# Triangular blocks through one load, their off-diagonal product in place, and a neighbour level inside a burst of small matmuls

## The chip, the cores and the metric

The kernel runs on one core of a Trainium2 chip. The metric is the device time of one execution in microseconds (us). A profile is one profiled execution: every instruction of TensorE (PE, with its weight loads PEld), VectorE (DVE), ScalarE (ACT), GpSimd (POOL) and every DMA issue on SyncE's queue (SPq), with start and duration.

## The reference

One decoder layer over 1024 prompt tokens and 8 sample tokens, all in float32. Cut to what the change touches:

```python
p = x @ w_in                                    # 1024 -> 9360 columns: GLA, RWKV-7, gates
# GLA (4 heads, keys 128, values 256): gated linear attention, in chunks
A = einsum('bhid,bhjd,bhijd->bhij', q, k, decay)   # decay = exp(b_i - b_j) for j <= i
o = A @ v + (q * exp(b)) @ S
# RWKV-7 (16 heads of 64): one state update per token
S = S * w_t + (S @ -kk_t) (kk_t * a_t)^T + v_t k_t^T ;  y_t = S @ r_t
...
m = sigmoid(gate_a) * (o_gla @ w_up_gla) + sigmoid(gate_b) * (o_rwkv @ w_up_rwkv)
y = layernorm(alpha * x + m @ w_out)
```

## The kernel before

The tokens go through in two passes of 512 (the 8 sample tokens ride with the first). The bulk of TensorE's work is `x @ w_in`: blocks of 128 columns, 24 matmuls each for a token tile, with x and w split into a rounded high and a low part (tiles `xs`, `wpart`, results in the PSUM tags `proj`, `big`, `pY`). Between these stand the two recurrences as side streams:

- RWKV (8 pairs of heads a pass, 16 in all): `pair` runs `front`, `back`, `turn`, `chain`, `norm`. A chunk of 64 tokens needs the inverse of a unit lower triangular 64x64 matrix. It is built from 32x32 blocks: the diagonal blocks of `GG` go to DRAM (`LD`) and come back as `L`, one matrix to a partition; VectorE solves them by 31 steps on `X`/`Xt`; the results go out to `XD` and come back as the diagonal of `XT` and as `X2`. The lower left block is a product of three: the off-diagonal block of `GG` (here carried by own transfers into `L1`), the transposed first inverse (`X1`, in which VectorE puts transposes into a zeroed block diagonal), and the second inverse (`X2`). The two products are the matmuls `big<-X,L` (out of it comes `A`) and `big<-X,A`.
- GLA (4 heads a pass, 8 in all): `gla_head` builds the 128x128 attention of a chunk by levels 1, 2, 4, ... 64: at level m, queries and keys that lie m apart. Level 0 (a token with itself) and level 1 (its neighbour) are products on VectorE, summed by a transpose and a reduce into `pair` tiles; levels 2 to 32 are 40 matmuls with 32 stationary columns in one burst (`big<-row`, 80 rows in a profile, since a float32 matmul shows as two), out of which predicated copies pick into `AC`.

The order on every engine is set when the program is built, by a greedy planner (`Order.run`): every stream offers its next operation, the planner's own costs say which could start first, priorities break ties, and each engine then executes its list in order. Any edit of a stream so moves the operations of all others a little. All DMAs are issued from one queue, SyncE's, in that order. The buffers are the tags of the table `SBUF` with a count each; `E.` operations may go to VectorE or GpSimd, `C.` operations to ScalarE or VectorE, as the planner sees fit. `slow` adds to the landing time that the planner reckons with; `together` issues several matmuls as one operation, its second argument scaling the planned cost.

Of the kernel before, what the change touches and what calls it, by code (L numbers as in the profile page):

```python
# [15 lines left out]
ALU = mybir.AluOpType  # L16
AP = bass.AP
# [3 lines left out]
P = 128  # L21
# [5 lines left out]
HT = TP // 2  # L27

PASS = [(0, HT + NS, NS, [(0, 256), (256, 264)]), (HT + NS, HT, 0, [(0, 512)])]
GH, GDK, GDV = 4, 128, 256  # L30
RH, RN = 16, 64
NPAIR = RH // 2
C = 64
NCH = HT // C
GC = 128
NGC = HT // GC
# [11 lines left out]
    "l2s": ([P, 2 * P], 1), "pc": ([P, NCH], 3), "X": ([P, 256], 1),  # L48
    "Xt": ([P, P], 1), "L1": ([P, P], 1), "A": ([P, P], 1), "S": ([P, GDV], 2), "Sp": ([P, C], 2), "s0p": ([P, C], 2), "rh": ([P, P], 2),
    "sto": ([P, P], 1), "az": ([P, 2 * HT], 2), "bnd": ([P, 1], 3), "st": ([P, 32], 3), "part": ([P, HALF], 2), "l2p": ([P, 2 * P], 2),  # L50
    "pair": ([P, 2, HT // 32], 3), "nst": ([P, 2 * NCH], 2), "ac": ([P, HT // 4], 1),
}
# [47 lines left out]
_o = 0  # L100
for _n, _w in [("ident", 128), ("gmask", 256)]:
    CST[_n] = (_o, _w)
    _o += _w
# [10 lines left out]
def constants():  # L114
    c = np.zeros((P, CST_W), np.float32)

    def put(name, v):
        o, w = CST[name]
        c[:, o:o + w] = v

    i = np.arange(P)
    put("ident", np.eye(P))
    s, t = i[:, None] % C, i[None, :] % C
    put("gmask", np.concatenate([s < t, s <= t], axis=1))
    j = np.arange(2 * B32) % B32
    lev = np.concatenate([i[:, None] % B32 // m == j // m for m in LEVELS[:MASKED]], axis=1).astype(np.uint8)
    return c, lev, ((i[:, None] // C) == (i[None] // C)).astype(np.float32)
# [295 lines left out]
class Kern(Order):  # L423
# [72 lines left out]
    def setup(self):  # L496
        nc, a = self.nc, self.a
        E = mybir.EngineType
# [59 lines left out]

        for tag, n, bufs in (("XT", 2 * HT, 2), ("X1", HT, 1), ("X2", HT, 1)):
            ts = [cp.tile([P, n], F32, name=f"{tag}{i}") for i in range(bufs)]  # L560
            for t in ts:
                nc.gpsimd.memset(t, 0.0)
            self.fixed(tag, ts)
# [235 lines left out]
    def gla_head(self, c, h, rows, g):  # L799
# [26 lines left out]
        u, w = z[:, :HT], vk1[:, :HT]  # L826
        r, r2, dd = yield from self.get("pair", 3)
        yield E.tensor_mul(u.rearrange("p (a e q) -> p a q e", e=2, q=GC), self.paired(q), self.paired(k))
        yield E.tensor_mul(qp_, qp_, al[:, :HT])
        yield V.transpose(w, u)  # L830
        yield V.tensor_reduce(r[:, 0], self.blocks32(w), mybir.AxisListType.X, ALU.add)
        half, four, two = NGC // 2, (4, HT // 4), [(2 * GC, NGC // 2), (2, GC // 2)]
        yield E.tensor_mul(self.strided(u, 0, *two, (GC + 1, 2)),
                           self.strided(km_, 0, (2 * GC, half), (4, GC // 2), (3, 2)),
                           self.strided(qp_, 2, (2 * GC, half), (4, GC // 2), (-1, 2)))
        yield V.transpose(w, u)
        yield V.tensor_reduce(r[:, 1], self.blocks32(w), mybir.AxisListType.X, ALU.add)
        b = [slice(32 * i, 32 * i + 32) for i in range(4)]
        for i in (0, 2):
            yield V.tensor_add(r2[b[i]], r[b[i]], r[b[i + 1]])  # L840
        for i in range(4):
            yield V.tensor_add(dd[b[i], :, 0:NGC], r2[b[0], :, i::4], r2[b[2], :, i::4])
        d0, d1 = (dd[:, i, 0:NGC].rearrange("p (a e) -> p a e", e=2).unsqueeze(2) for i in range(2))
        AC = yield from self.get("ac")
# [5 lines left out]
                                d0.to_broadcast([P, half, B32, 2]))  # L850
        yield V.copy_predicated(self.strided(AC, 2, (2 * B32, half), (4, B32 // 2), (-1, 2)),
                                eye.rearrange("p (b e) -> p b e", e=2).unsqueeze(1).to_broadcast([P, half, B32 // 2, 2]),
                                d1.to_broadcast([P, half, B32 // 2, 2]))
        self.free(r, r2, dd)
        kept = [z, vk1, *(yield from self.rows(2))]
        tot, pl = al[:, :HT], None
        small, mms = [m for m in LEVELS if 1 < m < B32], []
        for lv, m in enumerate(LEVELS):
# [8 lines left out]
            elif m == B32:  # L867
# [13 lines left out]
                for lo, y in enumerate(small):  # L881
                    yield V.copy_predicated(self.strided(AC, 2 * y, (4 * y, B32 // y), (1 - 2 * y, 2), (2, y)),
                                            lev[:, lo + 1].rearrange("p (b e m) -> p b e m", e=2, m=y),
                                            pl[:, lo].rearrange("p x (b e m) -> p (x b) e m", e=2, m=y))
# [250 lines left out]
    def front(self, c, p, st, d):  # L1135
# [80 lines left out]
        X = X_.rearrange("p (i t) -> p i t", t=32)  # L1216
        yield E.memset(X, 0.0)
        for q in range(4):
            yield E.memset(X_[NU * q:NU * q + NU, q::36], 1.0)
        for q in range(4):  # L1220
            yield slow(self.S.dma_start(L_[NU * q:NU * q + NU], LD.rearrange("n c s t -> (n c) (s t)")), 1.0)
        tm = yield from self.get("Xt")
# [12 lines left out]
        for q in range(4):  # L1235
            yield slow(self.S.dma_start(XD.rearrange("u (i g) t -> g u i t", g=4)[q], X[NU * q:NU * q + NU]), 0.5)
        self.free(X_)

        L1 = (yield from self.get("L1")).rearrange("p (x t) -> p x t", t=32)
        X2 = (yield from self.get("X2")).rearrange("p (g t) -> p g t", t=P)  # L1240
        H = NCH // 2
        for h in range(2):
            for n in range(2):
                g = 2 * h + n
                yield slow(self.S.dma_start(L1[32 * g:32 * g + 32], GG[64 * h:64 * h + 32, H * n:H * n + H, 0, h, 32:64]), -0.5)
        for q in range(2):
# [8 lines left out]
        d.AZ, d.BK, d.G, d.XT, d.v, d.bonus, d.pc, d.L, d.L1, d.X2 = AZ, BK, GG, XT, st[2], st[1], pc, L_, L1, X2  # L1255

    def back(self, d):
        GG, XT = d.G, d.XT

        H = NCH // 2  # L1260
        X1 = (yield from self.get("X1")).rearrange("p (x t) -> p x t", t=P)
        q = [slice(32 * n, 32 * n + 32) for n in range(4)]
        for h in range(2):
            for n in range(2):
                g = 2 * h + n
                yield self.V.transpose(X1[q[g], :, q[g]], XT[q[2 * h], H * n:H * n + H, h, 0:32])
# [575 lines left out]
```

## Time and profile before

| | us |
|---|---|
| median of 3 runs (lowest to highest) | 1476.96 (1476.38 to 1477.36) |
| the profiled execution | 1478.35 |
| its span, from the first to the last instruction | 1476.5 |
| PE busy in it | 1446.6 |
| DVE busy | 1163.0 |
| ACT busy | 878.9 |
| POOL busy | 108.8 |

The profiled execution took 1.85 us more than its span and 1.39 us more than the median of the runs. Nearly all operations are recorded by one helper line (L217), so a row is told by its tiles: `out<-in`, buffer numbers left out. A shape such as `128*32 128x32` in a PE row is the part of the array (rows*columns) and the operand moved (partitions x elements). "busy" counts time covered by any instruction of a group once; "mean ns" is the length of one instruction, which for pipelined matmuls is more than the time from one to the next.

### The profile page before, as it was taken

The page shows a single profiled execution, that of the slowest core. Times are in us where ns is not written, and L with a number is a line of the kernel's source. Part 1 is how long each engine was busy: PE and PEld are TensorE (multiplying, and loading weights), DVE is VectorE, ACT ScalarE, POOL GpSimd, SP SyncE. Part 2 cuts the span into 40 slices and gives each one's busy share as a digit, 9 for nine tenths or more (in the row PEclk, how much of TensorE's full clock was granted, in tenths as well). Part 3 has the DMA queues.
Part 4 walks back from the last instruction along what each step waited for, and adds up shares of the span by engine and source line. Part 5 has one row for each costly group of instructions (what it writes and reads, how often), then busy time and mean ns, then how long its engine had stood idle before and what let it go on. Part 6 is the DMA issues. An engine that isn't in the chain of part 4 may idle for free.

```text
span 1476.5 us, 31483 instructions
## 1 busy us (share of the span) xinstructions
PE 1446.6 (98%) x11158; PEld 1258.8 (85%) x11158; DVE 1163.0 (79%) x3071; ACT 878.9 (60%) x2302; POOL 108.8 (7%) x205
## 2 busy tenths in 40 slices
PE   9999999999999999999999999999999999999997
PEld 6999989999999998787878777778787899988786
DVE  6697879987899777967998898888876876755665
ACT  5666767775776677655775564465546746643210
POOL 1001010100110001000110210020000000000000
PEclk9999999999999999999999999999999999999999
DMA  8877887669765878548646457656654768987432
GB/s 308 278 260 228 260 268 239 215 212 313 259 240 193 289 259 269 174 140 249 207 131 198 148 160 240 205 153 172 182 172 142 246 196 253 295 300 258 135 109 84
DMA packets 211258, 318.96 MB, mean 216 GB/s; under 512 B 91811, under 2 KB 107180, under 8 KB 211100
## 3 DMA queue, kind: packets, MB, share of 16 engines
q1 hardware_dynamic: 211100, 316.93, 67.1%
q8 instruction: 89, 1.46, 0.4%
q14 instruction: 69, 0.57, 0.1%
HBM read 197.19 MB, written 118.61 MB: 214 GB/s over the span
## 4 chain that ended last, share of the span: by engine, by line
PE 77%; DVE 14%; ACT 3%; DMA 2%; issue 2%; SPq 1%; POOL 0%; POOLq 0%; DVEq 0%; ACTq 0%
PE proj L217 48%; PE big L217 20%; DVE row L217 6%; PE pch L217 5%; PE pY L217 4%; ACT row L217 2%; DVE X L217 1%; DVE wide L217 1%; DVE Xt L217 1%; SPq L217 1%; DVE pair L217 1%; ACT L401 1%; DVE az L217 1%; DVE bk L217 1%; DVE ac L217 1%
## 5 line engine op out<-in xcount | busy, mean ns | idle before, releaser
L217 PE MATMUL proj<-xs,wpart 128*128 128x264 f32 (+2 forms) x5640 | 1022.8, 327 | 1.0 <-DVE row L217 0.8
L217 PEld LDWEIGHTS proj<-xs,wpart 128*128 128x128 f32 x5640 | 811.2, 189 | 82.1 <-issue 10.3
L217 DVE TENSOR_TENSOR row<-row 128x512 f32<-128x512 f32 (+8 forms) x327 | 173.1, 537 | 13.0 <-ACT row L217 6.6
L217 ACT CAST wpart<-wraw 128x512 fp32r<-128x512 f32 x210 | 129.6, 622 | 89.7 <-PE proj L217 36.3
L217 DVE TENSOR_TENSOR wpart<-wraw,wpart 128x512 fp32r<-128x512 f32 x198 | 137.2, 695 | 34.4 <-ACT wpart L217 32.0
L217 ACT ACTIVATE row<-row 128x512 f32<-128x512 f32 (+3 forms) x197 | 117.6, 606 | 13.0 <-DVE row L217 4.1
L217 PE MATMUL big<-xs,wpart 128*128 128x512 f32 (+2 forms) x576 | 102.9, 332 | 0.8 <-DVE xs L217 0.7
L217 DVE TENSOR_TENSOR Xt<-X,wide 128x60 f32<-128x60 f32 (+21 forms) x432 | 94.7, 219 | 9.4
L217 ACT ACTIVATE row<-proj,omu 128x256 f32<-128x256 f32 (+1 forms) x99 | 54.0, 546 | 77.7 <-PE proj L217 77.2
L217 POOL TENSOR_TENSOR row<-row 128x512 f32<-128x512 f32 (+7 forms) x58 | 60.2, 1043 | 536.7 <-DVE row L217 190.5
L217 DVE TENSOR_TENSOR X<-X,Xt 128x60 f32<-128x60 f32 (+21 forms) x432 | 91.8, 212 | 9.7
L217 PEld LDWEIGHTS big<-xs,wpart 128*128 128x128 f32 x576 | 87.0, 191 | 11.9 <-DVE xs L217 1.6
L217 DVE SCALAR_TENSOR_TENSOR wide<-pch,pc,s0p 64x64 f32<-64x64 f32 x208 | 58.8, 283 | 41.6 <-PE pch L217 35.6
L217 ACT COPY rh<-pch 128x128 f32<-128x128 f32 x104 | 27.5, 264 | 84.8 <-PE pch L217 83.8
L401 ACT ACT_TABLE_LOAD x60 | 77.0, 1283 | 1.0
L217 DVE SCALAR_TENSOR_TENSOR row<-proj,pv,row 128x255 f32<-128x255 f32 (+1 forms) x99 | 56.4, 570 | 23.5 <-ACT tail L217 12.3
L217 ACT COPY row<-big 128x128 f32<-128x128 f32 (+7 forms) x144 | 41.1, 308 | 51.5 <-PE big L217 43.2
L217 PE MATMUL big<-row 128*32 128x32 f32 (+4 forms) x944 | 67.3, 243 | 0.8 <-ACT row L217 0.8
L217 ACT COPY row<-wide 64x64 f32<-64x64 f32 x240 | 58.2, 242 | 5.8 <-DVE wide L217 1.8
L217 ACT CAST xs<-row 128x520 fp32r<-128x520 f32 (+1 forms) x64 | 38.4, 622 | 29.2 <-PE proj L217 10.3
L217 PEld LDWEIGHTS pch<-wide,gg 128*128 128x128 f32 x256 | 41.9, 188 | 14.5 <-PE proj L217 5.6
L217 PE MATMUL pch<-wide,gg 128*128 128x128 f32 x256 | 51.2, 281 | 2.9 <-DVE wide L217 1.8
(252 smaller groups left out, 2008.9 us busy)
## 6 DMA issues: line engine op xcount, KB each, us to landing
w<-wpart SPq DMA_DIRECT2D x146, 512.0 KB
wpart<-w SPq DMA_DIRECT2D x146, 512.0 KB
wraw<-w_in SPq DMA_DIRECT2D x146, 256.0 KB
wide<-LD SPq DMA_DIRECT2D x64, 128.0 KB
wraw<-w_up_gla SPq DMA_DIRECT2D x32, 256.0 KB
wraw<-w_up_rwkv SPq DMA_DIRECT2D x32, 256.0 KB
sg<-row SPq DMA_DIRECT2D x16, 260.0 KB
row<-sg SPq DMA_DIRECT2D x16, 260.0 KB
```

The source lines that it names most:

```text
L217: ways.append((eng, lambda call=call: call(out, *args, **kw), price(eng, name, out, args, ins)))
L401: self.nc.scalar.preload_act_table_set(self.table)
```

## The change

1. **One load.** `L` was filled by four loads of the same DRAM matrices, each to 32 partitions, so that partition 32q+u held matrix u for q = 0 to 3. Now one load with a repeat of 4 in its source puts matrix u on partitions 4u to 4u+3, and the stores to `XD` read every fourth partition. The start value of `X`, formerly a memset and four small ones, is a copy of a new constant `unit`, which makes the constants 256 columns wider.
2. **In place.** The tile `L1` and its four transfers per pair go. The product is made by 16 matmuls with 32x32 blocks (before 4 with 128x32) that read the off-diagonal block of `GG` where it stands. `X1` is then a compact 256-column tile without zeroed blocks, filled by two transposes per pair for four, and the result is copied to `A` in two halves out of two banks.
3. **Level 1 in the burst.** `gla_head` drops the VectorE product, transpose, reduce and predicated copy of level 1; the level is two more copies of keys and queries and 8 more matmuls in the burst (48 for 40), with one more predicated copy out of its bank and one more `row` buffer held.

```diff
-for _n, _w in [("ident", 128), ("gmask", 256)]:
+for _n, _w in [("ident", 128), ("gmask", 256), ("unit", 256)]:
...
-        r, r2, dd = yield from self.get("pair", 3)
+        r, dd = yield from self.get("pair", 2)
...
-        yield E.tensor_mul(self.strided(u, 0, *two, (GC + 1, 2)),
-                           self.strided(km_, 0, (2 * GC, half), (4, GC // 2), (3, 2)),
-                           self.strided(qp_, 2, (2 * GC, half), (4, GC // 2), (-1, 2)))
-        yield V.transpose(w, u)
-        yield V.tensor_reduce(r[:, 1], self.blocks32(w), mybir.AxisListType.X, ALU.add)
...
-        yield V.copy_predicated(self.strided(AC, 2, (2 * B32, half), (4, B32 // 2), (-1, 2)),
-                                eye.rearrange("p (b e) -> p b e", e=2).unsqueeze(1).to_broadcast([P, half, B32 // 2, 2]),
-                                d1.to_broadcast([P, half, B32 // 2, 2]))
-        kept = [z, vk1, *(yield from self.rows(2))]
+        kept = [z, vk1, *(yield from self.rows(3))]
-        small, mms = [m for m in LEVELS if 1 < m < B32], []
+        small, mms = [m for m in LEVELS if m < B32], []
...
-        yield E.memset(X, 0.0)
-        for q in range(4):
-            yield E.memset(X_[NU * q:NU * q + NU, q::36], 1.0)
-        for q in range(4):
-            yield slow(self.S.dma_start(L_[NU * q:NU * q + NU], LD.rearrange("n c s t -> (n c) (s t)")), 1.0)
+        yield self.C.copy(X_, self.cst("unit"))
+        yield slow(self.S.dma_start(L_, AP(LD.tensor, LD.offset, [[1024, NU], [0, 4], [1, 1024]])), 1.0)
...
-            yield slow(self.S.dma_start(XD.rearrange("u (i g) t -> g u i t", g=4)[q], X[NU * q:NU * q + NU]), 0.5)
+            yield slow(self.S.dma_start(XD.rearrange("u (i g) t -> g u i t", g=4)[q], X[q::4]), 0.5)
-        L1 = (yield from self.get("L1")).rearrange("p (x t) -> p x t", t=32)
...
-                yield slow(self.S.dma_start(L1[32 * g:32 * g + 32], GG[64 * h:64 * h + 32, H * n:H * n + H, 0, h, 32:64]), -0.5)
...
-        X1 = (yield from self.get("X1")).rearrange("p (x t) -> p x t", t=P)
+        X1 = (yield from self.get("X1")).rearrange("p (c t) -> p c t", t=32)
         for h in range(2):
-            for n in range(2):
-                g = 2 * h + n
-                yield self.V.transpose(X1[q[g], :, q[g]], XT[q[2 * h], H * n:H * n + H, h, 0:32])
-        pA = yield from self.bank("big", [P, P])
-        yield together([self.P.matmul(pA[q[x]], d.L1[:, x], X1[:, x], start=True, stop=True) for x in range(H)])
+            yield self.V.transpose(X1[q[2 * h]], XT[q[2 * h], :, h, 0:32])
+        pA = yield from self.get("big", 2)
+        yield together([self.P.matmul(pA[h][q[x], 32 * n:32 * n + 32], GG[q[2 * h], H * n + x, 0, h, 32:64], X1[q[2 * h], H * n + x],
+                                      start=True, stop=True) for n in range(2) for x in range(H) for h in range(2)], 2.0)
         A_ = yield from self.get("A")
-        yield self.C.copy(A_, pA)
+        for h in range(2):
+            yield self.C.copy(A_[:, C * h:C * h + C], pA[h][:, :C])
```

TensorE, the second pair of the first pass: `big<-X,L` and then `big<-X,gg` is the product that makes `A`, `big<-X,A` the one that follows; `big<-az,bk`, `big<-part,headsr` and `big<-cons,bk` are other steps of the pairs. Before:

```order
L217 MATMUL proj<-xs,wpart 128x264 x6
L217 MATMUL big<-X_173,L_2811 32x128 x4
L217 MATMUL proj<-xs,wpart 128x264 x2
L217 MATMUL big<-az,bk 128x128 x8
L217 MATMUL proj<-xs,wpart 128x264 x12
L217 MATMUL big<-X_175,A 32x128 x4
L217 MATMUL proj<-xs,wpart 128x264 x2
L217 MATMUL big<-row 32x256 x4
```

Now:

```order
L218 MATMUL proj<-xs,wpart 128x264 x22
L218 MATMUL big<-X_2899,gg 32x32 x16
L218 MATMUL proj<-xs,wpart 128x264 x2
L218 MATMUL proj<-xs,wpart 128x256 x9
L218 MATMUL big<-part,headsr 128x512
L218 MATMUL proj<-xs,wpart 128x256 x5
L218 MATMUL big<-X_173,A 32x128 x4
L218 MATMUL big<-part,headsr 128x512
```

Four matmuls became sixteen; some 16 projection matmuls still stand between the two products.

SyncE's queue, the same pair: `XD<-X` stores the solved blocks, `L<-gg` are the four transfers of the off-diagonal block, `XT<-XD` and `X<-XD` load the inverses (`X` is here the tile `X2`), `wraw` and `w_0`/`w_1` are the weights of the projection. Before:

```order
L217 DMA XD_2784<-X 256x1x32 x4
L217 DMA L_2811<-gg 32x4x32 x4
L217 DMA wraw<-w_in 128x512
L217 DMA w_0_2773<-wpart 128x1024
L217 DMA XT_170<-XD_2784 32x8x32 x4
L217 DMA X_175<-XD_2784 32x4x32
L217 DMA wraw<-w_in 128x512
L217 DMA w_1_2898<-wpart 128x1024
L217 DMA X_175<-XD_2784 32x4x32
L217 DMA wraw<-w_in 128x512
L217 DMA w_0_2936<-wpart 128x1024
L217 DMA X_175<-XD_2784 32x4x32 x2
```

Now:

```order
L218 DMA XD_2700<-X 256x1x32 x4
L218 DMA wraw<-w_in 128x512
L218 DMA w_1_2745<-wpart 128x1024
L218 DMA XT_170<-XD_2700 32x8x32 x4
L218 DMA X_173<-XD_2700 32x4x32 x2
L218 DMA wraw<-w_in 128x512
L218 DMA w_0_2862<-wpart 128x1024
L218 DMA X_173<-XD_2700 32x4x32 x2
```

The four transfers are gone, and one weight load with one weight store less stands between the first and the last load of `X2`.

More of the change, by code (lines that the diff above doesn't have):

```diff
@@ L48 @@
     "l2s": ([P, 2 * P], 1), "pc": ([P, NCH], 3), "X": ([P, 256], 1),
-    "Xt": ([P, P], 1), "L1": ([P, P], 1), "A": ([P, P], 1), "S": ([P, GDV], 2), "Sp": ([P, C], 2), "s0p": ([P, C], 2), "rh": ([P, P], 2),
+    "Xt": ([P, P], 1), "X1": ([P, 256], 1), "A": ([P, P], 1), "S": ([P, GDV], 2), "Sp": ([P, C], 2), "s0p": ([P, C], 2), "rh": ([P, P], 2),
     "sto": ([P, P], 1), "az": ([P, 2 * HT], 2), "bnd": ([P, 1], 3), "st": ([P, 32], 3), "part": ([P, HALF], 2), "l2p": ([P, 2 * P], 2),
-    "pair": ([P, 2, HT // 32], 3), "nst": ([P, 2 * NCH], 2), "ac": ([P, HT // 4], 1),
+    "pair": ([P, HT // 32], 2), "nst": ([P, 2 * NCH], 2), "ac": ([P, HT // 4], 1),
 }
@@ L122, in constants @@
     put("ident", np.eye(P))
+    put("unit", np.eye(32).reshape(8, 4, 32).transpose(1, 0, 2).reshape(1, 4, 256).repeat(32, 0).reshape(P, 256))
     s, t = i[:, None] % C, i[None, :] % C
@@ L556, in setup @@
         nc.vector.memset(self.reset[:, ::C], 0)
-        for tag, n, bufs in (("XT", 2 * HT, 2), ("X1", HT, 1), ("X2", HT, 1)):
+        for tag, n, bufs in (("XT", 2 * HT, 2), ("X2", HT, 1)):
             ts = [cp.tile([P, n], F32, name=f"{tag}{i}") for i in range(bufs)]
@@ L830, in gla_head @@
         yield V.transpose(w, u)
-        yield V.tensor_reduce(r[:, 0], self.blocks32(w), mybir.AxisListType.X, ALU.add)
-        half, four, two = NGC // 2, (4, HT // 4), [(2 * GC, NGC // 2), (2, GC // 2)]
-        yield E.tensor_mul(self.strided(u, 0, *two, (GC + 1, 2)),
-                           self.strided(km_, 0, (2 * GC, half), (4, GC // 2), (3, 2)),
-                           self.strided(qp_, 2, (2 * GC, half), (4, GC // 2), (-1, 2)))
-        yield V.transpose(w, u)
-        yield V.tensor_reduce(r[:, 1], self.blocks32(w), mybir.AxisListType.X, ALU.add)
+        yield V.tensor_reduce(r, self.blocks32(w), mybir.AxisListType.X, ALU.add)
+        half = NGC // 2
         b = [slice(32 * i, 32 * i + 32) for i in range(4)]
         for i in (0, 2):
-            yield V.tensor_add(r2[b[i]], r[b[i]], r[b[i + 1]])
+            yield V.tensor_add(r[b[i]], r[b[i]], r[b[i + 1]])
         for i in range(4):
-            yield V.tensor_add(dd[b[i], :, 0:NGC], r2[b[0], :, i::4], r2[b[2], :, i::4])
-        d0, d1 = (dd[:, i, 0:NGC].rearrange("p (a e) -> p a e", e=2).unsqueeze(2) for i in range(2))
+            yield V.tensor_add(dd[b[i], 0:NGC], r[b[0], i::4], r[b[2], i::4])
+        d0 = dd[:, 0:NGC].rearrange("p (a e) -> p a e", e=2).unsqueeze(2)
         AC = yield from self.get("ac")
@@ L850, in gla_head @@
                                 d0.to_broadcast([P, half, B32, 2]))
-        yield V.copy_predicated(self.strided(AC, 2, (2 * B32, half), (4, B32 // 2), (-1, 2)),
-                                eye.rearrange("p (b e) -> p b e", e=2).unsqueeze(1).to_broadcast([P, half, B32 // 2, 2]),
-                                d1.to_broadcast([P, half, B32 // 2, 2]))
-        self.free(r, r2, dd)
-        kept = [z, vk1, *(yield from self.rows(2))]
+        self.free(r, dd)
+        kept = [z, vk1, *(yield from self.rows(3))]
         tot, pl = al[:, :HT], None
-        small, mms = [m for m in LEVELS if 1 < m < B32], []
+        small, mms = [m for m in LEVELS if m < B32], []
         for lv, m in enumerate(LEVELS):
@@ L882, in gla_head @@
                     yield V.copy_predicated(self.strided(AC, 2 * y, (4 * y, B32 // y), (1 - 2 * y, 2), (2, y)),
-                                            lev[:, lo + 1].rearrange("p (b e m) -> p b e m", e=2, m=y),
+                                            lev[:, lo].rearrange("p (b e m) -> p b e m", e=2, m=y),
                                             pl[:, lo].rearrange("p x (b e m) -> p (x b) e m", e=2, m=y))
@@ L1235, in front @@
         for q in range(4):
-            yield slow(self.S.dma_start(XD.rearrange("u (i g) t -> g u i t", g=4)[q], X[NU * q:NU * q + NU]), 0.5)
+            yield slow(self.S.dma_start(XD.rearrange("u (i g) t -> g u i t", g=4)[q], X[q::4]), 0.5)
         self.free(X_)
-        L1 = (yield from self.get("L1")).rearrange("p (x t) -> p x t", t=32)
         X2 = (yield from self.get("X2")).rearrange("p (g t) -> p g t", t=P)
         H = NCH // 2
-        for h in range(2):
-            for n in range(2):
-                g = 2 * h + n
-                yield slow(self.S.dma_start(L1[32 * g:32 * g + 32], GG[64 * h:64 * h + 32, H * n:H * n + H, 0, h, 32:64]), -0.5)
         for q in range(2):
@@ L1254, in front @@
             yield self.S.dma_start(X2[b, :, b], XD[2 * NCH + x::H].rearrange("g s t -> s g t"))
-        d.AZ, d.BK, d.G, d.XT, d.v, d.bonus, d.pc, d.L, d.L1, d.X2 = AZ, BK, GG, XT, st[2], st[1], pc, L_, L1, X2
+        d.AZ, d.BK, d.G, d.XT, d.v, d.bonus, d.pc, d.L, d.X2 = AZ, BK, GG, XT, st[2], st[1], pc, L_, X2
     def back(self, d):
@@ L1260, in back @@
         H = NCH // 2
-        X1 = (yield from self.get("X1")).rearrange("p (x t) -> p x t", t=P)
+        X1 = (yield from self.get("X1")).rearrange("p (c t) -> p c t", t=32)
         q = [slice(32 * n, 32 * n + 32) for n in range(4)]
         for h in range(2):
-            for n in range(2):
-                g = 2 * h + n
-                yield self.V.transpose(X1[q[g], :, q[g]], XT[q[2 * h], H * n:H * n + H, h, 0:32])
-        pA = yield from self.bank("big", [P, P])
-        yield together([self.P.matmul(pA[q[x]], d.L1[:, x], X1[:, x], start=True, stop=True) for x in range(H)])
+            yield self.V.transpose(X1[q[2 * h]], XT[q[2 * h], :, h, 0:32])
+        pA = yield from self.get("big", 2)
+        yield together([self.P.matmul(pA[h][q[x], 32 * n:32 * n + 32], GG[q[2 * h], H * n + x, 0, h, 32:64], X1[q[2 * h], H * n + x],
+                                      start=True, stop=True) for n in range(2) for x in range(H) for h in range(2)], 2.0)
         A_ = yield from self.get("A")
-        yield self.C.copy(A_, pA)
-        self.free(pA, X1, d.L1)
+        for h in range(2):
+            yield self.C.copy(A_[:, C * h:C * h + C], pA[h][:, :C])
+        self.free(*pA, X1)
         pZ = yield from self.bank("big", [P, H, 32])
```

## The prediction

> **What bounds the kernel now.** I read the page first: the busy times, the slices, the chain.
>
> ```profile
> span 1476.5 us, 31483 instructions
> PE 1446.6 (98%) x11158; PEld 1258.8 (85%) x11158; DVE 1163.0 (79%) x3071; ACT 878.9 (60%) x2302; POOL 108.8 (7%) x205
> PE   9999999999999999999999999999999999999997
> PEclk9999999999999999999999999999999999999999
> PE 77%; DVE 14%; ACT 3%; DMA 2%; issue 2%; SPq 1%; POOL 0%; POOLq 0%; DVEq 0%; ACTq 0%
> L217 PE MATMUL proj<-xs,wpart 128*128 128x264 f32 (+2 forms) x5640 | 1022.8, 327 | 1.0 <-DVE row L217 0.8
> ```
>
> TensorE is covered for 1446.6 of 1476.5 us, in every slice but the last, at full clock. Most of that is the projection, whose 5640 matmuls waited 1.0 us in all. The planner puts it wherever a recurrence waits, so a chain that becomes shorter gives nothing by itself. What can change the time is work added to or taken from TensorE, and its idle time: 1476.5 - 1446.6 = 29.9 us. A piece of that is the end of the program. From the timeline of PE, the last row:
>
> ```profile
> 1468.24 0.52 PE L217 MATMUL proj<-wpart,xs 128*128 128x256 f32 x3
> ```
>
> It ends at 1468.8, so 7.7 us are the last layer norm and its stores, which the change leaves alone. Some 22.2 us of waits remain in the whole program. I then asked for the groups by form, and for the timeline around the two products that the change touches:
>
> ```profile
> L217 PE MATMUL big<-X,L 128*32 128x128 f32 x128 | 6.8, 284 | 3.1 <-issue 1.8 <-DVE X L217 1.3
> L217 PE MATMUL big<-X,A 128*32 128x128 f32 x128 | 6.8, 285 | 2.8 <-DMA X<-XD 2.1 <-DVE A L217 0.6
> ```
>
> The two products of the pairs carry 3.1 + 2.8 = 5.9 us of the 22.2. The other 16.3 us are scattered over the rest of the streams.
>
> **The change part by part.** The sum is made against the profiled execution (1478.35 us) and is a difference, which I then put on the median of the runs, 1.39 us lower.
>
> *The burst of GLA (on the path).* Eight matmuls, 16 rows, are added in each of 8 heads. One burst and its successor:
>
> ```profile
> 93.65 0.91 PE L217 MATMUL big<-row 128*32 128x32 f32 x80
> 94.48 3.46 PE L217 MATMUL proj<-xs,wpart 128*128 128x264 f32 x27
> ```
>
> From start to next start 0.83 us for 80 rows, 10.4 ns each. 16 x 10.4 = 0.17 us a head, 8 heads: **+1.3 us**. The new matmuls have the form of those 80, so I give this no range of its own.
>
> *The product that makes A (on the path).* Per pair 8 rows of 128 moved columns go, and 32 rows of 32 moved columns come. The trace has no matmul on 32x32 of the array; these are its neighbours:
>
> ```profile
> 189.27 0.43 PE L217 MATMUL big<-X,L 128*32 128x128 f32 x8
> 189.63 0.51 PE L217 MATMUL proj<-xs,wpart 128*128 128x264 f32 x2
> ...
> 195.02 0.43 PE L217 MATMUL big<-X,A 128*32 128x128 f32 x8 [2.12 <-DMA X<-XD]
> ...
> 196.38 0.71 PE L217 MATMUL big<-cons,bk 64*128 64x64 f32 x16
> 197.02 0.76 PE L217 MATMUL proj<-xs,wpart 128*128 128x264 f32 x4
> ```
>
> Before, 189.63 - 189.27 = 0.36 us. The nearest row is the GLA burst: the same 32 stationary and 32 moved columns, only 128 rows deep for 32. At its 10.4 ns, 32 rows take 0.33 us, 0.03 less, 16 pairs: **-0.5 us**. That is the value I take. The low end: the new form has two row blocks working beside each other where the burst has one, so at half the price 0.17 us, 16 x -0.19 = -3.0. The high end: the 64x64 transposes, a more remote form, take 197.02 - 196.38 = 0.64 us for 16 rows, 40 ns each; 32 of them 1.28 us, 16 x 0.92 = +14.7.
>
> The Trainium skill, "TensorE: Matmul & The Clock Gate", section "Wait — 56ns, not 53.3ns?", says that start-to-start of matmuls never falls below about 25 ns however few columns are moved; by it 32 rows would take 0.8 us and this term would be +7.0 us in place of -0.5 (an estimate from the page's figure). The burst above, at 10.4 ns a row, lies far under that floor, so the trace disagrees for matmuls on different column blocks, and the sum goes by the trace.
>
> *Waits of TensorE on these two products.* The wait of 2.1 us has its cause in SyncE's queue. Its timeline around there, and the tile rows of the DMAs:
>
> ```profile
> 175.42 2.55 SPq L217 DMA_DIRECT2D XD<-X  x4
> 178.02 2.58 SPq L217 DMA_DIRECT2D L<-gg  x4
> ...
> 181.81 2.56 SPq L217 DMA_DIRECT2D XT<-XD  x4
> ...
> 187.94 1.65 SPq L217 DMA_DIRECT2D X<-XD  x2
> L217 SPq DMA_DIRECT2D L<-gg x64: 585/600/1438, 107.9 to 1202.2; - x64
> L217 SPq DMA_DIRECT2D wide<-LD x64: 307/421/1338, 68.9 to 1159.4; - x64
> ```
>
> The four `L<-gg` held the queue for 2.58 us ahead of the loads that the product waited for. With them gone, 64 x 0.600 = 38 us of issue leave the queue, and 48 of the 64 loads of `L`, 48 x 0.421 = 20 us. So the 2.1 us should go. Of the 1.3 us behind `DVE X` I count 0.9 as gained (XT lands earlier and the transposes below are shorter). The 0.6 behind the copy to `A` stays, and the 1.8 of "issue" too, as no row says what they are: **-3.0 us**. Ends: 0, since the order is drawn anew and a load may be late elsewhere, and -5.9, all of it.
>
> *The elementwise work (beside other work).* Rows of the groups by form:
>
> ```profile
> L217 DVE TENSOR_TENSOR row<-row 128x256 f32<-128x256 f32 x119 | 50.8, 440 | 0.8
> L217 DVE STREAM_TRANSPOSE row<-row 128x512 f32<-128x512 f32 x16 | 11.3, 708 | 0.2
> L217 DVE TENSOR_REDUCE pair<-row 128x16 f32<-128x512 f32 x16 | 10.9, 683 | 0.2
> L217 DVE COPY_PREDICATED ac<-lev,pair 128x64 f32<-128x64 uint8 x8 | 2.4, 302 | 0.0
> L217 DVE COPY_PREDICATED ac<-lev,big 128x64 f32<-128x64 uint8 x32 | 9.6, 300 | 0.6
> L217 DVE COPY row<-row 128x256 f32<-128x256 f32 x25 | 6.9, 287 | 0.0
> L217 ACT COPY row<-row 128x256 f32<-128x256 f32 x47 | 19.1, 431 | 17.4 <-DVE row L217 16.9 <-POOL row L217 0.2
> L217 DVE STREAM_TRANSPOSE X<-XT 32x128 f32<-32x128 f32 x64 | 19.2, 300 | 3.0 <-DMA XT<-XD 2.2
> L217 ACT COPY A<-big 128x128 f32<-128x128 f32 x8 | 2.1, 265 | 9.2 <-PE big L217 9.2
> L217 ACT COPY wide<-pch 64x64 f32<-64x64 f32 x160 | 33.0, 206 | 22.9 <-PE pch L217 18.7
> L217 POOL MEMSET X<- 32x8 f32 x60 | 6.3, 105 | 3.1
> L217 POOL MEMSET X<- 128x256 f32 x15 | 5.2, 350 | 37.2 <-DMA XD<-X 37.1
> ```
>
> A head loses 0.440 + 0.708 + 0.683 + 0.302 = 2.13 us and gains a predicated copy of 0.300 and two copies of 0.287 (DVE) or 0.431 (ACT): 1.0 to 1.3 us less, about 9 us over 8 heads. A pair has four transposes of 0.300 for two of 256 columns (between the 300 ns of 128 and the 708 of 512, some 0.44): 0.3 us less, 5 us in all. The copy to `A` is two of about 0.21 for one of 0.265, 16 x 0.15 = 2.4 us more; the copy of `unit` adds 16 x 0.29 to 0.43 to DVE or ACT, some 6 us, and POOL loses 6.3 + 5.2 us. DVE so gives up some 10 of 1163 us. I cost all this at nothing: the projection covers it on TensorE. If that cover were gone, the pair's own path would be 0.15 us longer at the copies and 0.3 shorter at the transposes.
>
> *Other.* The constants are 128 KB larger and are loaded once; GLA and the pairs first need them tens of us later, behind projection. One more `row` of 33 is held in a head: at worst a block waits for a buffer, and the order shows no place where TensorE would stand without projection for it. Both 0.
>
> Sum: 1.3 - 0.5 - 3.0 = -2.2 us. Part of it I expect to see given back: all 16.3 us of the other waits are drawn anew with the order, which helps as often as it harms, so I leave that at 0 and put about 4 us (a quarter of them, an estimate) on either side of the range. Profiled 1478.35 - 2.2 = 1476.1; on the median 1476.96 - 2.2 = **1474.8 us**.
>
> **The rivals.** What a measurement of this kernel can tell from no change is about 0.2%, 3 us.
>
> 1. *Clearly faster*: all 5.9 us of waits go, and the 32x32 rows come at half price: 1.3 - 3.0 - 5.9 = -7.6, so 1469.4 us. For it: the queue loses 58 us of issue, and DVE and POOL have less to do. Against it: three waits of "issue" without a named cause.
> 2. *Slower by the price of small matmuls*: if a 32x32 row costs 40 ns like the 64x64 ones, the product costs +14.7 and the sum is 1.3 + 14.7 - 3.0 = +13.0, 1490.0 us. It decides from about 20 ns a row: 16 x 32 x (20 - 10.4) ns = 4.9 us, which turns -2.2 into +2.7. For it: 512 instructions of a form that the trace does not show. Against it: the burst. By the Trainium skill's floor of about 25 ns from the page named above, the sum would be 1482.3 us.
> 3. *Slower by a new wait*: the order is new, and a load that lands late leaves TensorE standing at a product as it stood 2.1 us at 195.0. Two such and none of the old ones gained: 1.3 - 0.5 + 4.2 = +5.0, 1482.0 us. For it: DVE and the queue are the planner's guesses; against it: 5640 projection matmuls waited only 1.0 us.
> 4. *The change moves nothing*: the freed queue and DVE time is covered as before and the waits stay at 5.9: +0.8, 1477.8 us.
>
> **How the numbers follow.** The forecast, together with rival 4, which lies within its spread: 0.50; rival 1: 0.32; rival 2: 0.08; rival 3: 0.10. A part of the forecast's own spread (0.04) falls below -3 us. So faster 0.36, same 0.45, slower 0.19. The range is from rival 1 with a little beyond, 1468.5, to just short of rival 3, 1481.5; rival 2 lies outside.
>
> **What the profile after would show.** The rows `L<-gg` gone, 16 loads `wide<-LD`; bursts of 96 rows at about 1.0 us to the next start; 512 rows `big<-X,gg`, 0.33 us from a burst's start to the next row; idle before them and before `big<-X,A` under 3 us in sum for 5.9; DVE busy near 1150, POOL near 95. PE's idle total near 27 us. I would be wrong if bursts of 32 take over 0.6 us, or if PE's waits elsewhere grow by more than 4 us.

## The result and the profile after

The changed kernel takes 1466.22 us (median of 6 runs, 1464.59 to 1471.07), the kernel before 1477.16 us beside it (6 runs, 1475.17 to 1478.82). The ratio is 0.9927 [0.9917, 0.9938]: 10.9 us faster, where the forecast was 2.2 us with a range that ended at 1468.5. The forecast was wrong: right in sign, and 8.6 us above the measured time. The profiled execution took 1466.08 us.

From the page of the kernel after (the span, busy times by engine, the costliest group):

```profile
span 1464.1 us, 32120 instructions
PE 1443.8 (99%) x11670; PEld 1261.4 (86%) x11670; DVE 1139.0 (78%) x3022; ACT 888.7 (61%) x2356; POOL 77.7 (5%) x107
...
L218 PE MATMUL proj<-xs,wpart 128*128 128x264 f32 (+2 forms) x5640 | 1018.3, 327 | 1.0 <-DVE row L218 0.8
```

The span is 12.4 us shorter. PE's idle time went from 29.9 to 20.3 us (-9.6), and PE's busy time fell by 2.8 us although it has 512 rows of matmuls more (a float32 matmul shows as two rows). That second figure is not less work, as the accounting below shows. The projection waited 1.0 us, as before. The two products, from the groups by form (busy, mean ns | idle time ahead and what ended it):

```profile
L218 PE MATMUL big<-X,A 128*32 128x128 f32 x128 | 7.2, 285 | 0.5 <-DMA X<-XD 0.5
L218 PE MATMUL big<-X,gg 32*32 32x32 f32 x512 | 6.2, 196 | 0.4 <-DVE X L218 0.4
```

Their idle time is 0.9 us for 5.9. Two bursts and the last row, from the timeline of PE (start, length):

```profile
87.58 1.03 PE L218 MATMUL big<-row 128*32 128x32 f32 x96
88.54 0.63 PE L218 MATMUL proj<-xs,wpart 128*128 128x264 f32 x3
...
183.47 0.35 PE L218 MATMUL big<-X,gg 32*32 32x32 f32 x32
183.75 0.52 PE L218 MATMUL proj<-xs,wpart 128*128 128x264 f32 x2
...
186.62 0.42 PE L218 MATMUL big<-X,A 128*32 128x128 f32 x8 [0.48 <-DMA X<-XD]
...
1455.97 0.52 PE L218 MATMUL proj<-wpart,xs 128*128 128x256 f32 x3
```

From start to next start the GLA burst takes 0.96 us for 96 rows, the new product 0.28 us for 32 rows. Seven of the 8 GLA bursts take 0.96 to 1.01 us and one, with a wait inside, 2.27; of the 16 bursts of the product 13 take 0.28 to 0.29 us, and three have a wait inside (0.46, 0.54 and 0.75 us). The end behind the last projection is as long as before. SyncE's queue, the same pair:

```profile
170.55 2.89 SPq L218 DMA_DIRECT2D XD<-X  x4
...
176.07 1.83 SPq L218 DMA_DIRECT2D XT<-XD  x4
177.95 0.93 SPq L218 DMA_DIRECT2D X<-XD  x2
...
181.09 1.50 SPq L218 DMA_DIRECT2D X<-XD  x2
```

The four `L<-gg` are gone, and the loads of the inverses stand closer behind the stores. Over the 16 pairs, the mean time from the first store to `XD` to the first load of `XT` fell from 6.7 to 4.9 us, and to the start of the first product from 12.9 to 11.7 us.

Five of the larger waits of PE (us in total, times, longest), before:

```profile
PE pch L217 <- DVE wide L217: 3.3, 8, 0.9
PE big L217 <- DMA X<-XD: 2.1, 1, 2.1
...
PE big L217 <- DVE part L217: 1.7, 4, 0.7
...
PE big L217 <- DVE S L217: 1.6, 2, 1.3
...
PE big L217 <- DVE l2p L217: 1.3, 2, 0.9
```

And after:

```profile
PE pch L218 <- DVE wide L218: 1.6, 5, 0.4
PE big L218 <- DVE part L218: 1.4, 2, 1.1
...
PE big L218 <- DVE S L218: 0.4, 1, 0.4
```

Waits shrank in places where the change edits nothing: `pch` and `part` belong to the chain of RWKV, `S` is the state of GLA.

**An account that does not trust "busy".** A matmul's modelled end runs over the next one's start (mean length 406 ns for the widest projection, 232 ns from start to start), so a wait of up to some 0.17 us counts as busy, and a longer one in part. I therefore took every matmul's start from the trace. Its time to the next start, less the usual step of its form (the median where the same form follows, the smaller of the two kernels'), is time lost. Summed, in us:

| | before | after | change |
|---|---|---|---|
| steps at their usual length (the work) | 1331.6 | 1334.6 | +3.0 |
| lost ahead of the two products | 9.3 | 4.0 | -5.3 |
| lost ahead of the pairs' chain (`pch`, `part`, `l2p`) | 25.0 | 17.5 | -7.5 |
| lost between two projections | 50.0 | 47.9 | -2.1 |
| lost elsewhere | 50.9 | 50.4 | -0.5 |
| ahead of the first matmul and from the last one's start | 9.8 | 9.7 | -0.1 |
| span | 1476.5 | 1464.1 | -12.4 |

So the gain is in lost time: 5.3 us at the products that the change edits, 7.5 us at the chain that it does not edit. Not all lost time is a wait that another order would save: between two projections some 42 us, in either kernel, are about 470 steps that are each some 0.09 us too long. What changed most are the long steps: those more than 0.5 us beyond the usual were 29 before, 24.4 us in sum, and are 17 after, 12.7 us. Of the work's +3.0 some 2.2 are bookkeeping: timed as whole bursts, start to next start, the GLA bursts cost 1.0 us more (8 x 0.13) and those of the new product 0.2 less (5.5 us for 5.7), +0.8 in sum, and the difference is credited in the row "elsewhere".

One piece of the loss is the clock. From the windows of the kernel before and, below it, of the kernel after (us, PE, PEld, DVE, ACT, POOL busy, granted clock, DMA share, GB/s):

```profile
1200.00:1300.00 100.00, 97.99 (x791) 92.19 (x790) 66.20 (x139) 57.32 (x123) 0.00 (x0) 0.98 0.82 261
1225.00:1235.00 10.00, 8.79 (x54) 7.89 (x54) 7.88 (x19) 6.32 (x16) 0.00 (x0) 0.83 0.77 244
```

```profile
1200.00:1300.00 100.00, 99.14 (x748) 92.15 (x749) 64.41 (x127) 59.08 (x129) 0.00 (x0) 1.00 0.84 277
```

Before, waits around 1230 us were followed by one stretch of 3.41 us at half clock, which costs at most 1.7 us of work (the projection's usual step of 122 ns takes 220 ns in it). After, there is none while the projection runs. The row `PEclk`, all nines, hid it: a slice of it is 37 us.

### The profile page after: what moved, and what is told of

It reads as the page before. It is cut to its first block, busy times and chain, and to the rows that moved or that the text cites. A ratio compares the mean times of both kernels' runs of the same rounds, so it can differ in the third digit from the quotient of the medians.

```text
span 1464.1 us, 32120 instructions
## 1 busy us (share of the span) xinstructions
PE 1443.8 (99%) x11670; PEld 1261.4 (86%) x11670; DVE 1139.0 (78%) x3022; ACT 888.7 (61%) x2356; POOL 77.7 (5%) x107
## 5 line engine op out<-in xcount | busy, mean ns | idle before, releaser
L218 DVE TENSOR_TENSOR row<-row 128x512 f32<-128x512 f32 (+8 forms) x331 | 169.6, 521 | 8.3 <-ACT row L218 2.6
L218 DVE TENSOR_TENSOR wpart<-wraw,wpart 128x512 fp32r<-128x512 f32 x203 | 141.7, 700 | 34.5 <-ACT wpart L218 32.6
L218 ACT ACTIVATE row<-row 128x512 f32<-128x512 f32 (+5 forms) x197 | 119.0, 607 | 17.8 <-DVE row L218 8.2
L218 DVE TENSOR_TENSOR X<-X,Xt 128x60 f32<-128x60 f32 (+21 forms) x432 | 95.5, 221 | 9.2
L218 DVE TENSOR_TENSOR Xt<-X,wide 128x60 f32<-128x60 f32 (+21 forms) x432 | 91.5, 212 | 8.8
L218 PEld LDWEIGHTS big<-xs,wpart 128*128 128x128 f32 x576 | 87.0, 188 | 11.8 <-DVE xs L218 1.1
L218 POOL TENSOR_TENSOR row<-row 128x512 f32<-128x512 f32 (+6 forms) x46 | 49.9, 1090 | 631.2 <-DVE row L218 279.9
L218 PE MATMUL pch<-wide,gg 128*128 128x128 f32 x256 | 50.9, 280 | 2.0 <-DVE wide L218 1.3
L218 ACT ACTIVATE row<-proj 128x128 f32<-128x128 f32 (+4 forms) x136 | 37.1, 326 | 25.8 <-PE proj L218 24.9
```

Source lines behind the costliest of these rows:

```text
L218: ways.append((eng, lambda call=call: call(out, *args, **kw), price(eng, name, out, args, ins)))
```

## The experiments

Three theories. **A**: the gain comes from work taken off DVE and off SyncE's queue. **B**: it comes from the order, which any edit draws anew, and other draws would give other times. **C**: it comes from the product in place, that is from its form and from the transfers that it no longer needs. Each run below is against the kernel before on the same chip, 1477 to 1478.5 us.

**Each part alone.** `p_load` is part 1 of the diff alone, `p_place` part 2, `p_gla` part 3:

```diff
# p_load, in the kernel before
-        yield E.memset(X, 0.0)
-        for q in range(4):
-            yield slow(self.S.dma_start(L_[NU * q:NU * q + NU], ...), 1.0)
+        yield self.C.copy(X_, self.cst("unit"))
+        yield slow(self.S.dma_start(L_, AP(LD.tensor, LD.offset, [[1024, NU], [0, 4], [1, 1024]])), 1.0)
# p_place, in the kernel before
-                yield slow(self.S.dma_start(L1[...], GG[...]), -0.5)
-        yield together([self.P.matmul(pA[q[x]], d.L1[:, x], X1[:, x], ...) for x in range(H)])
+        yield together([self.P.matmul(pA[h][...], GG[...], X1[...], ...) for n in range(2) for x in range(H) for h in range(2)], 2.0)
# p_gla, in the kernel before
-        yield V.transpose(w, u)
-        yield V.tensor_reduce(r[:, 1], self.blocks32(w), mybir.AxisListType.X, ALU.add)
-        small, mms = [m for m in LEVELS if 1 < m < B32], []
+        small, mms = [m for m in LEVELS if m < B32], []
```

> The kernel before with part 1 alone (one load of L, the constant for X, every fourth partition stored). Theory A (the waits of TensorE shrink because the queue and the elementwise engines have less to do, each part giving its share): 48 issues and the POOL memsets go, so about 2 to 4 us faster, 1473 to 1475. Theory B (the new order is a lucky draw): anywhere within 5 us of the kernel before, in either direction. Theory C (the waits at the product that makes A, and its transfers, were the cost): unchanged within 2 us, since the transfers into L1 stay.

> The kernel before with part 2 alone (the product in place, no L1 transfers, compact X1). Theory A: 64 issues and 5 us of transposes go, 2 to 5 us faster. Theory B: anywhere within 5 us, either way. Theory C: this part carries most of the 11 us, 1466 to 1470, and the rows of the product and of big<-X,A wait under 2 us in sum for 5.9.

> The kernel before with part 3 alone (level 1 of GLA in the burst). Theory A: DVE gives up some 9 us, TensorE gains 1.3 us of work, so 2 to 5 us faster. Theory B: anywhere within 5 us, either way. Theory C: 1 us slower, since the pairs' products are as before.

Measured: `p_load` 1490.93 us, ratio 1.0086 [1.0071, 1.0100]; `p_place` 1468.26, 0.9928 [0.9914, 0.9942]; `p_gla` 1485.44, 1.0056 [1.0037, 1.0076]. Part 2 alone shows the whole gain, as C had it, though the two products still wait 2.9 us there, where C had less than 2. `p_load` and `p_gla` lie outside the ranges of all three theories. Part 1 takes 48 loads and the memsets out, puts one copy a pair in, and is 12.4 us slower. The waits of PE in `p_load`:

```profile
PE pch L218 <- DVE wide L218: 4.3, 8, 2.0
PE big L218 <- DMA row<-o_rwkv: 3.5, 1, 3.5
PE big L218 <- ACT part L218: 3.2, 3, 2.6
PE big L218 <- DMA w<-wpart: 2.1, 1, 2.1
```

These are single waits of 2 to 3.5 us in places that part 1 does not edit. They also cost clock. Windows of `p_load`, columns as above:

```profile
755.00:765.00 10.00, 7.08 (x101) 5.16 (x102) 9.80 (x41) 8.37 (x15) 0.00 (x0) 0.93 0.40 120
765.00:775.00 10.00, 8.14 (x31) 5.92 (x32) 9.86 (x30) 6.84 (x18) 0.00 (x0) 0.84 0.29 68
1200.00:1300.00 100.00, 94.21 (x808) 91.05 (x808) 66.34 (x150) 57.30 (x129) 0.00 (x0) 0.97 0.76 244
```

Stretches at half clock begin at 763.5, 773.8 and 1220.9 us, at most 6.8 us of lost work together. A reading by A alone cannot give a slower `p_load`.

**The same operations in another order.** In the planner, a random number of up to 0.01 us either way is added to the key by which it picks the next operation, so that near ties fall otherwise:

```diff
+        self.rng = np.random.default_rng(1)      # 2 in the second draw
...
+                    key += self.rng.uniform(-0.01, 0.01)
                     if best is None or key < best[0]:
```

> The kernel before, with the same operations, but the planner adds a random number within 0.01 us to every key, so that near-ties fall otherwise and most of the order is drawn anew. Theory A: the same operations cost the same within 2 us, 1475 to 1479, and all waits of TensorE stay near 22 us. Theory B: the draws scatter as much as the change moved, some 5 to 10 us, and this one can lie anywhere from 1466 to 1487.

> The kernel before, a second random draw of near-ties (within 0.01 us). Theory B: anywhere from 1466 to 1491. Theory C: with the product and its transfers as before, again some 1475 to 1491.

> The changed kernel, a first random draw of near-ties (within 0.01 us). Theory B: the changed kernel's 1466 was a good draw, so a new one lies anywhere from 1466 to 1491, most likely near 1480. Theory C: within 5 us of the changed kernel, 1462 to 1472.

> The changed kernel, a second random draw. As for the first: theory B anywhere from 1466 to 1491, theory C 1462 to 1472.

Measured: the kernel before, redrawn, 1485.22 (1.0045 [1.0029, 1.0061]) and 1479.79 us (1.0017 [1.0000, 1.0033]); the kernel after, redrawn, 1468.02 (0.9937 [0.9922, 0.9952]) and 1468.86 us (0.9937 [0.9921, 0.9954]). So the order alone makes the old kernel 6.7 and 2.8 us slower than it was on the same chip, and moves the new one by some 1.5 us, and the kernels after stay faster in every draw: the means of three draws are 1480.7 us before and 1467.7 us after, 13.0 us apart. In the slowest draw of the old one the loss stands at the product itself (groups by form):

```profile
L217 PE MATMUL big<-X,L 128*32 128x128 f32 x128 | 7.0, 292 | 10.7 <-DMA XT<-XD 6.2 <-DVE X L217 2.2 <-issue 1.5
```

A caution on all redraws, the three further down too: the random order leaves out something that the planner's own order keeps. In all of them but `a_draw2` the outputs `y` are not the layer's, while the states of GLA and RWKV are. They have as many matmuls and DMA issues as the kernels that they redraw, so they compare the same amount of work; presumably some operation of the late stages runs ahead of one that it needs. Which one, and what keeping it in its place would cost, is not known.

**Two parts of three**, for the effect of each part over all settings of the others; `m_load_gla` is parts 1 and 3, and so on, with the same edits:

```diff
# m_load_gla: kernel after, with part 2 as before
-        yield together([self.P.matmul(pA[h][...], GG[...], X1[...], ...) ...], 2.0)
+        yield together([self.P.matmul(pA[q[x]], d.L1[:, x], X1[:, x], ...) for x in range(H)])
# m_load_place: level 1 of GLA as before
# m_place_gla: the four loads and the memsets as before
```

> Parts 1 and 3 without part 2 (no product in place). Theory B (any edit redraws the order, and the draw makes the time): anywhere from 1466 to 1491, not tied to what the parts were alone. Theory C (the product in place is what pays, in whatever order): near the two parts alone and the redrawn kernel of before, 1482 to 1492, 15 us and more over the whole change.

> Parts 1 and 2, without part 3. Theory B (the draw of the order makes the time): anywhere from 1466 to 1491. Theory C (the product in place pays in whatever order): 1463 to 1472.

> Parts 2 and 3, without part 1. Theory B: anywhere from 1466 to 1491. Theory C: 1463 to 1472.

Measured: `m_load_gla` 1469.42 us, 0.9943 [0.9926, 0.9959]; `m_load_place` 1474.21, 0.9978 [0.9966, 0.9991]; `m_place_gla` 1475.43, 0.9991 [0.9976, 1.0005]. All three lie outside the ranges of C, the first far below it, the other two 2 to 3 us above. Parts 1 and 3, each slower alone, give 8 us together without part 2. The parts do not add. Averaged over the eight combinations, part 2 is worth -9.7 us (1471.0 with it, 1480.7 without), part 1 -1.4 and part 3 -3.5. With the scatter of the draws, each such figure is uncertain by about 4 us, so only part 2's stands out.

**Work put back on the engines and the queue.** From here on C is split in two: by C1 only waiting for the transfers to land cost time, by C2 the transfers themselves do. In the kernel after, its results unread: level 1's product, transpose and reduce on VectorE (`a_dve`); the four transfers of `L1` (`a_l1`); four loads of `L` to every fourth partition in place of one (`a_load4`); the transfers and the four loads together (`a_queue`).

```diff
# a_dve
+        yield E.tensor_mul(self.strided(u, 0, *two, (GC + 1, 2)), ...)
+        yield V.transpose(w, u)
+        yield V.tensor_reduce(rx, self.blocks32(w), mybir.AxisListType.X, ALU.add)
# a_l1, a_queue
+                yield slow(self.S.dma_start(L1[32 * g:32 * g + 32], GG[64 * h:64 * h + 32, H * n:H * n + H, 0, h, 32:64]), -0.5)
# a_load4, a_queue
-        yield slow(self.S.dma_start(L_, AP(LD.tensor, LD.offset, [[1024, NU], [0, 4], [1, 1024]])), 1.0)
+        for q in range(4):
+            yield slow(self.S.dma_start(L_[q::4], LD.rearrange("n c s t -> (n c) (s t)")), 1.0)
```

> The changed kernel with the elementwise work of level 1 put back (product, transpose and reduce into a tile that nothing reads; the level itself stays in the burst), some 15 us of DVE work. Theory A (TensorE waits less because DVE has less to do): 3 to 8 us slower than the changed kernel, 1469 to 1474, with more waits of the chain's matmuls on DVE. Theory C: within 4 us of the changed kernel, 1463 to 1470.

> The changed kernel with the DMA issues put back: the four transfers into L1 are issued at their old place but nothing reads L1, and L is loaded by four DMAs (to every fourth partition each). Theory C1 (the product no longer has to wait until the transfers have landed): still 1463 to 1472, and the rows of the two products wait as little as in the changed kernel. Theory C2 (the 58 us of issue on SyncE's queue and the small transfers themselves were the cost): back towards 1477 to 1485.

> The changed kernel with only the four transfers into L1 put back, unread; one load of L. Theory C2 (the transfers hold SyncE's queue and the DMA engines ahead of the loads that the product waits for): the loss at the two products back near 11 to 13 us for 6.6, the time 1471 to 1481. Theory C1 (only waiting for their landing cost): the loss stays at 6 to 9, the time 1464 to 1475.

> The changed kernel with L loaded by four DMAs again, no transfers into L1. Theory C2: as the changed kernel, loss at the products 6 to 9 us, time 1464 to 1475. If the single load was what paid: loss at the products 10 to 13 us, time 1472 to 1482.

Measured: `a_dve` 1465.97 us, 0.9925 [0.9907, 0.9942]; `a_queue` 1478.67, 1.0018 [1.0001, 1.0036]; `a_l1` 1473.66, 0.9979 [0.9969, 0.9988]; `a_load4` 1470.67, 0.9957 [0.9940, 0.9974]. The page of `a_dve` shows that the work is back:

```profile
PE 1443.2 (99%) x11670; PEld 1262.4 (86%) x11670; DVE 1144.3 (78%) x3039; ACT 890.0 (61%) x2356; POOL 84.6 (6%) x116
```

Five more microseconds on DVE and seven on POOL cost nothing that shows in this one order: the elementwise half of A falls, within the scatter of a draw. The transfers, unread, take the gain away, all of it in `a_queue` and two thirds in `a_l1`. I had looked for their cost at the products. Groups by form of `a_queue`:

```profile
L218 PE MATMUL big<-X,gg 32*32 32x32 f32 x512 | 7.5, 196 | 5.2 <-DVE X L218 5.0
```

and of `a_l1`:

```profile
L218 PE MATMUL big<-X,gg 32*32 32x32 f32 x512 | 6.4, 196 | 0.5 <-DVE X L218 0.4
L218 PE MATMUL big<-X,A 128*32 128x128 f32 x128 | 6.8, 285 | 0.8 <-DMA X<-XD 0.8
```

In `a_queue` 5.2 us do stand there, in `a_l1` 1.3, and `a_l1` is still 7.4 us slower than the kernel after. By the account above, `a_l1` loses 4.2 us ahead of the products (after: 4.0), but 28.9 ahead of the chain (17.5). Up to 3.4 us of its loss is clock: its trace has a stretch of 6.83 us at half clock from 859.6 us. The loss at the products in the expectations is by another count, which takes in the steps inside the bursts: 12.6 us before, 6.6 after. By it `a_queue` has 12.7, `a_l1` 6.5 and `a_load4` 5.4 us: the loss that C2 foretold came about in `a_queue` alone.

**Is it the draw again?** `a_queue` and `a_l1` with the planner redrawn; and the converse, the old product without transfers: `b_copy` is the kernel before with `L1` filled by four copies on ScalarE or VectorE, also redrawn.

```diff
# b_copy, b_copy_draw1
-                yield slow(self.S.dma_start(L1[32 * g:32 * g + 32], GG[64 * h:64 * h + 32, H * n:H * n + H, 0, h, 32:64]), -0.5)
+                yield self.C.copy(L1[32 * g:32 * g + 32], GG[64 * h:64 * h + 32, H * n:H * n + H, 0, h, 32:64])
# a_queue_draw1, a_l1_draw1, b_copy_draw1
+                    key += self.rng.uniform(-0.01, 0.01)
```

> The changed kernel with the transfers into L1 (unread) and the four loads put back, in a random draw of near-ties (within 0.01 us). Theory C2: loss at the products again 10 to 15 us, time 1472 to 1485. Theory C1: loss 6 to 9 us, time 1464 to 1475, and the first such kernel was a bad draw.

> The changed kernel with the four unread transfers into L1, in a random draw of near-ties. If the transfers cost something in any order: 1472 to 1480 again, above the 1466 to 1471 of most kernels of the new form without them. If only the form of the product matters: 1464 to 1475.

> The kernel before, with its old product from L1, but L1 filled by four engine copies of 32x128 in place of the four transfers. Theory C2 and C1 alike: the loss at the products falls from 12.6 to 6 to 9 us and the time to 1466 to 1476, though ScalarE or VectorE get 64 copies more. If the new form of the product was what paid: loss 10 to 15 us, time 1475 to 1490.

> The old form of the product with L1 filled by engine copies, in a random draw of near-ties (within 0.01 us). If the form of the product is what pays, and not the transfers: 1477 to 1490 again. If the transfers are what pays and the first such kernel was a bad draw: 1464 to 1475.

Measured: `a_queue_draw1` 1477.07 us, 1.0000 [0.9988, 1.0012]; `a_l1_draw1` 1478.44, 1.0007 [0.9998, 1.0017]; `b_copy` 1486.13, 1.0079 [1.0053, 1.0105]; `b_copy_draw1` 1485.79, 1.0064 [1.0047, 1.0081]. By that other count `a_queue_draw1` loses 7.8 us at the products, `a_l1_draw1` 6.6, `b_copy` 10.1: the times are those of C2, the losses at the products are not, and `b_copy` is 10 us above what C1 and C2 alike foretold. `b_copy` by form:

```profile
L217 PE MATMUL big<-X,A 128*32 128x128 f32 x128 | 6.8, 285 | 0.0
L217 PE MATMUL big<-X,L 128*32 128x128 f32 x128 | 6.8, 284 | 3.2 <-DVE X L217 3.1
```

The wait for `X<-XD` of 2.1 us, which the prediction put down to the four transfers ahead of it, is gone without them. That shows little, since it is gone with the transfers in place too in `b_draw2`, `p_load` and `m_load_gla`: it hangs on the draw. And the kernel is 9 us slower: by the account it loses 30.6 us ahead of the chain, where the kernel before loses 25.0, and 56.6 elsewhere, where that loses 50.9. That the 64 copies more on ScalarE and VectorE cause it is possible, but not shown; the other reading is that the old form of the product, and not its transfers, is what costs there.

All kernels by the form of the product:

| product, transfers of `L1` | kernels | us | mean |
|---|---|---|---|
| old, read | before, `p_load`, `p_gla`, `b_draw1`, `b_draw2`, `m_load_gla` | 1469.4 to 1490.9 | 1481.3 |
| old, copies in their place | `b_copy`, `b_copy_draw1` | 1485.8, 1486.1 | 1486.0 |
| new, unread | `a_l1`, `a_l1_draw1`, `a_queue`, `a_queue_draw1` | 1473.7 to 1478.7 | 1477.0 |
| new, none | after, `p_place`, `a_draw1`, `a_draw2`, `m_load_place`, `m_place_gla`, `a_dve`, `a_load4` | 1466.0 to 1475.4 | 1469.7 |

The kernels of a row scatter by a standard deviation of 7.5 (first row), 2.3 (third) and 3.5 us (last); the means are so uncertain by 3.1, 1.2 and 1.2. Between none and unread transfers lie 7.3 us, with 1.7 of uncertainty: that is shown, for the new form (two of the four kernels with transfers have 48 more loads of `L` besides). Between old with transfers and new with unread ones lie 4.3 us, with 3.3: that may be the draw. Between old with copies and new with none lie 16.3 us: no run here has the old form with neither transfers nor copies, so what the form itself is worth stays open. No kernel was faster than the kernel after by more than its interval; `a_dve` equals it.

**What stays open.** Where the 7.3 us of the transfers arise. The loss ahead of the products is 4.4 us in the mean of the last row and 5.1 in the third, that ahead of the chain 23.5 and 25.8, that elsewhere 46.6 and 49.1, that between projections 48.6 and 49.5: a little everywhere, not at one consumer. Half clock has little part in it: up to 1.5 us a kernel in the last row and 2.1 in the third. Whether it is SyncE's time (its issues took 567 us after, 615 in `a_l1`), the transfers' traffic or the place that they take in the plan was not told apart.

## Why the prediction was wrong

**What bounds the kernel** was read rightly: the work on TensorE and its waits. The work grew by 3.0 us at usual steps, and all of the gain is lost time that shrank.

**The GLA burst** was right: 0.96 us for 96 rows where 0.83 stood for 80, 8 x 0.13 = +1.0 us for a forecast of +1.3 (the wait inside one burst left aside).

**The product that makes A** came a little cheaper than priced: 0.28 us where no wait stands inside, forecast 0.33. With the waits inside three bursts it is 0.34 us in the mean of 16 (5.5 us in all; before 5.7), -0.2 us for the forecast -0.5. Rival 2, 40 ns a row and 1490.0 us, is refuted. The Trainium skill, "TensorE: Matmul & The Clock Gate", section "Wait — 56ns, not 53.3ns?", with its floor of about 25 ns from start to start, would have 0.8 us here; the trace has 8.8 ns a row in the burst shown and disagrees, as it did for the GLA burst.

**Waits on the two products**: direction and place were right, the size was not. Idle time ahead of them fell from 5.9 to 0.9 us, -5.0 for the forecast -3.0: the 1.8 of "issue", which I had kept because no row named its cause, went too. By starts it is -5.3. This belongs to rival 1. It is not one draw: over the six kernels of the table's first row the idle time ahead of the two products is 6.1 us in the mean (2.8 to 12.2), over the eight of its last row 1.4 us (0.4 to 3.1). The cause that the prediction named, the four transfers ahead of `X<-XD`, is not shown: that wait comes and goes with the draw.

**The elementwise work** was rightly costed at nothing. DVE fell to 1139.0 (forecast 1150) and POOL to 77.7 (forecast 95), and in `a_dve` putting work back there cost nothing that shows.

**The step that failed** is the one behind the sum: "all 16.3 us of the other waits are drawn anew with the order, which helps as often as it harms, so I leave that at 0 and put about 4 us (a quarter of them, an estimate) on either side". It is mis-sized in three ways.

1. The draw is wider. The same operations redrawn gave 6.7 and 2.8 us more than the kernel before on the same chip, and part 1 alone, 48 loads fewer, 12.4 us more. A quarter of 16.3 us was too narrow for the range.
2. Its mean is not 0. Three draws of each kernel lie 13.0 us apart in the mean, so the measured 10.9 us are not the luck of one order, and by the account above the time lost outside the products falls by some 9 us between these means (from about 124 to about 115, of which 2.2 are again the bookkeeping). Transfers put back unread cost 7.3 us in the mean of the comparison above, only 0.7 of it at the products; the prediction priced them only where a row showed their consumer waiting, 2.1 us. By what path they reach the other waits stays open.
3. The 16.3 us were the wrong base. Idle time of PE shows only the waits that outlast a modelled end. It fell outside the products from 16.3 to 20.3 - 7.6 - 0.9 = 11.8 us (7.6 is the end, 1464.1 - 1456.5), by 4.5. By starts the time lost outside them fell from 125.9 to 115.8 us, by 10.1, of which 2.2 are the bookkeeping named above: 7.9.

The clock, which the prediction took as full, gave up to 1.7 us of these 7.9. Put together against the span: work +0.8 (forecast +0.8), the products' waits -5.3 (forecast -3.0), waits elsewhere with the clock -7.9 (forecast 0): -12.4 us.

Rival 1 was nearest, 1469.4 us for 1466.2, and right in one of its two means: the waits of the products went, but the 32x32 rows did not come at half price (0.28 us a burst for 0.17). Rival 3 did not come about in the kernel after; `p_load` shows that its mechanism is real, with waits of 2 to 3.5 us in new places. Rival 4 is refuted.

## What to carry to other kernels

Where a planner orders everything, one measured edit is one draw: redraw near ties at random in both kernels, two or three times each, before a few microseconds are credited to an edit, and take the spread as the width of the forecast. A transfer on the one DMA queue can cost more than the waits of its own consumer: here transfers without a consumer cost 7.3 us. And where TensorE is 98% busy, count time from start to start of its matmuls as well: the busy share hides the shorter waits, and the idle time shows only 9.6 of the 12.4 us here.

## What the runs showed of the hardware

- The granted clock halves for stretches of 3.41 us (or two or three of them), and not only after a whole idle stretch. In the 3.41 us just ahead of one, PE was covered for 2.38 us in the kernel before, for 1.40 ahead of the first in `p_load` and for 0.51 in `b_draw1` (in this order, columns as above):

```profile
1228.05:1231.46 3.41, 2.38 (x12) 1.57 (x11) 2.31 (x5) 2.60 (x7) 0.00 (x0) 1.00 0.97 315
760.13:763.54 3.41, 1.40 (x54) 0.84 (x58) 3.21 (x14) 3.39 (x9) 0.00 (x0) 1.00 0.50 154
1194.48:1197.90 3.42, 0.51 (x5) 0.29 (x3) 2.33 (x4) 1.28 (x2) 0.00 (x0) 1.00 0.18 29
```

  One stretch costs at most 1.7 us of work, `p_load` paid up to 6.8 and `b_draw1` up to 5.1. The Trainium skill, "TensorE: Matmul & The Clock Gate", section "What's actually happening", gives a window of 4096 cycles at 1.2 GHz, 3413 ns, and half or full rate and nothing between; the trace agrees with both: every stretch at half clock that a trace here has between the matmuls is 3.41 us or two or three times that, and no other rate occurs.
- Sixty-four transfers of 16 KB that nothing reads cost 7.3 us (1.7 of uncertainty) in the mean of four kernels against eight, where no instruction waits for them.
